# Up's weight sums in place, and a fixed VectorE order in the last part of a two-layer trunk kernel

## The chip, the cores and the metric

The kernel runs on 1 core of one Trainium2 chip. The metric is the device time of one execution in microseconds (us), on the slowest core, which here is the only one. The core's engines are TensorE (PE in the profile, its weight loads PEld), VectorE (DVE), ScalarE (ACT), GpSimd (POOL) and SyncE (SP, which here only starts transfers). Each takes its instructions in the order that the compiler wrote down, and an instruction that waits holds up those behind it.

## The reference

A two-layer decoder trunk over 512 positions of 1024 channels, in float32. Each layer adds a mixer to the residual and then a gated feed-forward part (FFN) to it; a root-mean-square norm stands before each, and one at the end. The change lies in the two FFNs, and in the end of the second:

```
def gated_conv_ffn(x, w_gate, w_up, conv_w, conv_b, w_down):
    g = jnp.einsum('bsd,df->bsf', x, w_gate)
    g = causal_dwconv3(g, conv_w) + conv_b
    up = jnp.einsum('bsd,df->bsf', x, w_up)
    return jnp.einsum('bsf,fd->bsd', jax.nn.silu(g) * up, w_down)
...
    hn = rms_norm(h, norm_ffn[layer])
    h = h + gated_conv_ffn(hn, w_ffn_gate[layer], w_ffn_up[layer], conv_ffn[layer],
                           b_conv_ffn[layer], w_ffn_down[layer])
return rms_norm(h, final_norm)
```

The hidden width is 2816, which is 22 blocks of 128.

## The kernel before, in words

**Three products for one.** Each float32 operand is split into a high part, rounded to TensorE's float32r, and a low part, the rest. A product is then the sum of high by high, high by low and low by high. A split costs a copy on ScalarE (high) and a subtraction on VectorE (low); in another form (`summed`, lines 136 to 145, and `split` in `prepare`, lines 753 to 758) ScalarE writes the negated rounded copy, and a DMA started by GpSimd adds the original to it on its way (`accum_op`), which spares VectorE.

**Seven products for eight.** From block 2 on, the FFN's hidden blocks are made in pairs (f = 2, 4, ..., 20, each f and f+1) by a Winograd scheme: a 2 by 2 product of sub-blocks is done with seven products of sums and differences. `prepare(f)` (line 729) loads four raw tiles (Gate and Up, each in two halves of the input channels; four buffers "raw"), and forms for each of Gate ("g") and Up ("u") two tiles of sums: s12 (lines 744 to 748, for products 5 and 6) and s34 (lines 767 to 769, for products 7 and 3). The tiles of sums carry the tag "sum", which has three slots; the compiler gives a tile a slot once all readers of the tile that had it are done. Each is split into high and low parts (L726 and L727, or for Gate from f = 6 on by ScalarE and the accumulating DMA, L756 to L758). `behind(a, b)` only says that a comes after b on the same engine: the sums of a stage come after the last stage's add of product 7 (`self.added`).

`products(f)` (line 779) then runs fourteen products in the order g1, u1, g5, g2, g6, u5, u6, u2, g7, u7, g3, u3, g4, u4. They accumulate in a few PSUM banks (a, b, e; `BANK`, line 552): product 6 goes on top of product 1 in bank a, so it may start only when ScalarE has copied product 1 out (L810) and, from f = 6 on, where the bank holds two halves, VectorE has added the second half (L798). After g3 and g4 come the scale by the norm's factor (L822), the convolution (`conv`, L610 on ScalarE, two steps L612 on VectorE) and silu (L620), after u4 the gating (L830 to L837).

**Order of stages.** `steps` runs the stages f = 0, 2, 4, ..., 20, and after some of them a half of the down projection of four finished blocks (`half_down`; d in layer 0, dn in layer 1), whose results VectorE adds to the residual (L313 in layer 0, L1181 in layer 1). The stage f = 6 is the first wide one.

**The last part of layer 1** (from line 1201). The last four hidden blocks (rows 18 to 21) go through the down projection by the same seven products, now with the hidden blocks as sums too. The raw weights are b11, b12, b21, b22; `less` forms the differences (L1218; t1 and t2, called dnt in the profile, lie in "sum" slots), and `put` splits each weight operand (`stat`) by ScalarE and an accumulating DMA (tiles whi_dnp and wlo_dnp). `block` (line 1233) splits the activations' operands: blocks 1 and 2 are the rows a11 and a12, blocks 5 and 6 the sums s1 and s2 (called dns), blocks 3, 7 and 4 come from a12, a21 and a22 (high on ScalarE, low on VectorE, L1237 to L1243). The products run in the order that the calls of `taken` have: each is six matmuls into a bank followed by VectorE's add to y (L1181). Products 1, 6, 7 and 4 of one half of the tokens share a bank, so product 6 waits for the add after product 1. `inorder` keeps an instruction in the order of the program among the others on its engine that are marked so; everything else the compiler places by its own reckoning. Then come squares, roots and the final scale, row block by row block, and the output DMAs.

Of the kernel before, what the change touches and what calls it, by code (L numbers as in the profile page):

```python
# [8 lines left out]
F32 = mybir.dt.float32  # L9
F32R = mybir.dt.float32r  # L10
BF16 = mybir.dt.bfloat16
AF = mybir.ActivationFunctionType
ALU = mybir.AluOpType
PSUM = bass.MemoryType.PSUM

P = 128
D = 1024
S = 512
# [3 lines left out]
NF = FF // P  # L22
# [9 lines left out]
def tile_trunk(ctx: ExitStack, tc: tile.TileContext, x, norm_mix, norm_ffn, final_norm,  # L32
# [3 lines left out]
    nc = tc.nc  # L36
    x = x[0]
# [45 lines left out]
    def behind(ins, first):  # L83

        if first is not None:
            tc.add_manual_dep(ins.ins, first.ins.name, mybir.DependencyInfo(
                mybir.DependencyClass.NoSync, mybir.DependencyReason.DATA), reason="order")
# [500 lines left out]
    class Ffn:  # L588
# [10 lines left out]
        def __init__(self, layer, prm, norm, ap, sums):  # L599
            self.layer, self.prm, self.ap, self.acts = layer, prm, ap, {}  # L600
            self.norm, self.sums = norm, sums
            self.t23, self.t41, self.t41both = {}, {}, {}
            self.first_sums = None
            self.added = {"g": None, "u": None}
            self.cols = small[:, 3 * PAD : 3 * PAD + NT]

        def conv(self, t, ft):
            ap, prm, n = self.ap, self.prm, f"{self.layer}_{ft}"
            c = ap.tile([P, S], F32, tag="c", bufs=2, name=f"c{n}")
            nc.scalar.activation(c, t[:, 0:S], AF.Copy, scale=prm("cf", ft))  # L610
            for i in (1, 2):
                nc.vector.scalar_tensor_tensor(c, t[:, i : S + i], prm("cf", i * NF + ft), c,  # L612
                                               op0=ALU.mult, op1=ALU.add)
            return c

        def silu(self, c, ft):
            name = f"s{self.layer}_{ft}"
            s = (self.ap.tile([P, S], F32, tag="s", bufs=3, name=name) if ft % 2 else
                 tp.tile([P, S], F32, tag="sq", name=name))
            nc.scalar.activation(s, c, AF.Silu, bias=self.prm("bf", ft))  # L620
            return s

        def act(self, ft, s):
# [105 lines left out]
        def prepare(self, f):  # L729
# [11 lines left out]
                put(key, 1, w, i)  # L741
            for key in "gu":
                r0, r1 = raws[key, 0][0], raws[key, 1][0]
                s12, s34 = (ap.tile([P, 2, 4, P], F32, tag="sum", bufs=3, name=f"{x}{key}_{n}")
                            for x in ("s12", "s34"))
                behind(nc.vector.tensor_tensor(s12[:, 0], r0[:, :, P:], r1[:, :, P:], ALU.add),
                       self.added[key])
                nc.vector.tensor_tensor(s12[:, 1], s12[:, 0], r0[:, :, :P], ALU.subtract)
# [404 lines left out]
    def ffn1(norm):  # L1153
        with tc.tile_pool(name="f1", bufs=1) as ap:
# [59 lines left out]
            def put(product, how, src, **kw):  # L1214
                stat[product] = how(src, 2, 512, f"dnp{product}", **kw)

            def less(dst, x, y_):
                behind(nc.vector.tensor_tensor(dst, x, y_, ALU.subtract), ffn.added["u"])  # L1218

            less(t1, b12, b11)  # L1220
            put(1, summed, b11)
            put(2, summed, b21)
            less(t2, b22, t1)
            put(5, summed, t1)
            put(6, summed, t2)
            less(b12, b22, b12)
            put(3, summed, b22)
            put(7, summed, b12)
            less(b21, b21, t2)

            blocks = {}

            def block(product, n, srcs, after=None):
                hi, lo = (x.rearrange("p (a b) -> p a b", a=2) for x in hg[n])
                blocks[product] = hi, lo
                if not isinstance(srcs, list):
                    ins = nc.scalar.activation(hi, srcs, AF.Copy)  # L1237
                    behind(nc.vector.tensor_tensor(lo, srcs, hi.bitcast(F32), ALU.subtract), after)
                    return ins
                for i, src in enumerate(srcs):  # L1240
                    ins = nc.scalar.activation(hi[:, i], src, AF.Copy)
                    behind(nc.vector.tensor_tensor(lo[:, i], src, hi[:, i].bitcast(F32),
                                                   ALU.subtract), after)  # L1243
                return ins

            a11, a12 = ([rows[a + 2 * i + n][:, :HALF] for n in range(2)] for i in range(2))
            a21, a22 = ([rows[a + 2 * i + n][:, HALF:] for n in range(2)] for i in range(2))
            s1, s2 = (ap.tile([P, 2, HALF], F32, tag="c", bufs=2, name=f"dns{i}") for i in (1, 2))
            block(1, 0, a11)
            block(2, 1, a12)  # L1250
            for n in range(2):
                nc.vector.tensor_tensor(s1[:, n], a21[n], a22[n], ALU.add)
            block(5, 4, s1)
            for n in range(2):
                nc.vector.tensor_tensor(s2[:, n], s1[:, n], a11[n], ALU.subtract)
            put(4, summed, b21, after=block(6, 5, s2))
            banks = {}

            def product(p, i, c0=0, c1=512, bank=None):
# [53 lines left out]
                queue.dma_start(out[t * P : (t + 1) * P, cs], dst)  # L1313


            first_add = taken(1, 0, left)
            for n in range(2):
                nc.vector.tensor_tensor(a12[n], a12[n], s2[:, n], ALU.subtract)
            last_split = block(3, 6, a12, first_add)
            for n in range(2):  # L1320
                nc.vector.tensor_tensor(a21[n], a11[n], a21[n], ALU.subtract)
            block(7, 2, a21, first_add)
            block(4, 3, a22, first_add)

            first_root = work("sd", 1, "first")
            behind(nc.scalar.activation(first_root, eps, AF.Sqrt), last_split)

            taken(1, 1, left)
            taken(2, 0, left)
            taken(5, 0, right)  # L1330
            squared(0, left)
            times(vec, 0, left)
            halved(0, left, True)
# [55 lines left out]
    n = mixer0()  # L1389
# [33 lines left out]
```

## Time and profile before

| what | value |
|---|---|
| time, median of 3 runs | 981.55 us (981.4 to 983.6) |
| the profiled execution's own time | 982.37 us |
| its span in the trace | 980.7 us |
| TensorE busy | 966.7 us (99%), granted clock 0.997 of full |
| VectorE busy | 815.2 us (83%), 1379 instructions |
| ScalarE busy | 593.8 us (61%) |
| GpSimd busy | 144.3 us (15%) |
| end of the last matmul | about 973.3 us |
| DMA | 146.01 MB, mean 149 GB/s |

The span is the profile's time from first to last record; some 1.7 us of the execution lie outside it. Matmul ends are modelled, so a busy TensorE says that matmuls were under way, and gaps show as idle time with the instruction that ended the wait. A row of the timeline has the start, the time taken, the engine, the line, the operation, the tile written and the tiles read, the shapes, the count, and in brackets the idle time of the engine before it with what released it.

### The profile page before, as it was taken

How to read it: one execution, taken by the hardware profiler on the slowest of the kernel's cores; microseconds unless marked ns; L12 is line 12 of the kernel's file. 1: busy time of each engine (PE TensorE's matmuls, PEld its weight loads, DVE VectorE, ACT ScalarE, POOL GpSimd, SP SyncE). 2: the span in 40 equal slices, each digit the busy share in tenths (PEclk: the TensorE clock that was granted, in tenths of full speed). 3: DMA queues.
4: the chain of work that ended last, by engine and by line, in shares of the span. 5: the costliest groups of instructions: out<-in, count | busy, mean ns of one | idle time of the engine just before them, and what ended most of it. 6: DMA issues, size and time to landing. Idle time of an engine off the chain costs nothing.

```text
span 980.7 us, 14161 instructions
## 1 busy us (share of the span) xinstructions
PE 966.7 (99%) x5200; PEld 832.1 (85%) x5200; DVE 815.2 (83%) x1379; ACT 593.8 (61%) x899; POOL 144.3 (15%) x167
## 2 busy tenths in 40 slices
PE   9999999999999999999999999999999999999996
PEld 7888888997888888888889988889978888888884
DVE  5887459979899898998987765489898989889887
ACT  5523347674676565765488734586765566655675
POOL 2141023010111010110310001310111011100122
PEclk9999999999999999999999999999999999999998
DMA  7442226566777678774324623265766877667774
GB/s 249 146 136 86 87 87 139 136 149 158 193 164 185 145 172 193 165 188 127 121 61 113 212 68 105 56 141 134 180 162 163 199 171 185 149 159 196 190 159 124
DMA packets 93554, 146.01 MB, mean 149 GB/s; under 512 B 5060, under 2 KB 60076, under 8 KB 93484
## 3 DMA queue, kind: packets, MB, share of 16 engines
q1 hardware_dynamic: 78316, 98.69, 32.0%
q0 software_dynamic: 13392, 44.57, 25.7%
q10 hardware_dynamic: 1776, 1.84, 0.6%
q8 instruction: 41, 0.67, 0.3%
q14 instruction: 29, 0.24, 0.1%
HBM read 98.42 MB, written 2.10 MB: 103 GB/s over the span
## 4 chain that ended last, share of the span: by engine, by line
PE 86%; DVE 5%; DMA 4%; issue 3%; POOL 0%; ACT 0%; POOLq 0%; DVEq 0%; ACTq 0%
DMA wlo_s12g<-s12g 3%; PE d L157 3%; PE d L156 3%; PE d L155 3%; PE dn L156 2%; PE dn L157 2%; PE dn L155 2%; PE gu L155 2%; PE gu L157 1%; PE oo L157 1%; PE gu L156 1%; PE oo L156 1%; PE oe L156 1%; PE oe L155 1%; PE oo L155 1%
## 5 line engine op out<-in xcount | busy, mean ns | idle before, releaser
L612 DVE SCALAR_TENSOR_TENSOR c<-rows,prm,c 128x512 f32<-128x512 f32 x88 | 65.4, 746 | 3.8 <-ACT c L610 3.6
L142 POOL DMA_DIRECT2D wlo_g<-raw_g x20 | 17.2, 862 | 341.1 <-ACT wlo_g L140 175.1
L156 PE MATMUL dn<-wlo_dn,a_hi 128*128 128x512 f32 x144 | 56.2, 390 | 0.0
L157 PE MATMUL dn<-whi_dn,a_lo 128*128 128x512 f32 x144 | 56.2, 390 | 0.0
L156 PE MATMUL d<-a_lo,whi_d 128*128 128x512 f32 x144 | 56.2, 390 | 0.0
L157 PE MATMUL d<-a_hi,wlo_d 128*128 128x512 f32 x144 | 56.1, 390 | 0.0
L155 PE MATMUL d<-a_hi,whi_d 128*128 128x512 f32 x144 | 56.1, 390 | 0.0
L155 PE MATMUL dn<-whi_dn,a_hi 128*128 128x512 f32 x144 | 56.1, 389 | 0.0
L726 ACT ACTIVATE whi_a<-raw_g 128x512 fp32r<-128x512 f32 x20 | 12.6, 632 | 61.6 <-PE g_6e L567 8.5
L620 ACT ACTIVATE s<-c,prm 128x512 f32<-128x512 f32 x44 | 31.4, 719 | 16.1 <-DVE c L612 16.1
L211 POOL TENSOR_TENSOR ssq_f<-ssq_f,sq_f 128x512 f32<-128x512 f32 x14 | 19.4, 1388 | 134.6 <-ACT sq_f L210 99.7
L200 ACT ACTIVATE hg<-h,prm 128x512 fp32r<-128x512 f32 x24 | 17.3, 722 | 35.0 <-DVE h L313 35.0
L610 ACT ACTIVATE c<-rows,prm 128x512 f32<-128x512 f32 x44 | 31.3, 713 | 2.9 <-DVE rows L822 2.8
L201 DVE SCALAR_TENSOR_TENSOR hg<-h,prm,hg 128x512 fp32r<-128x512 f32 x24 | 23.6, 987 | 11.1 <-ACT hg L200 11.1
L157 PEld LDWEIGHTS dn<-whi_dn,a_lo 128*128 128x128 f32 x144 | 27.0, 188 | 5.7
L157 PEld LDWEIGHTS d<-a_hi,wlo_d 128*128 128x128 f32 x144 | 27.0, 188 | 5.7
L155 PEld LDWEIGHTS dn<-whi_dn,a_hi 128*128 128x128 f32 x144 | 27.0, 188 | 5.4
L156 PEld LDWEIGHTS dn<-wlo_dn,a_hi 128*128 128x128 f32 x144 | 27.0, 188 | 5.4
L155 PEld LDWEIGHTS d<-a_hi,whi_d 128*128 128x128 f32 x144 | 27.1, 188 | 5.4
L156 PEld LDWEIGHTS d<-a_lo,whi_d 128*128 128x128 f32 x144 | 27.0, 188 | 5.4
L264 ACT ACTIVATE a_hi<-s 128x512 fp32r<-128x512 f32 x40 | 24.8, 627 | 10.8 <-PE d L157 7.2
L151 DVE TENSOR_TENSOR wlo_dn<-raw_dn,whi_dn 128x1024 fp32r<-128x1024 f32 x18 | 22.0, 1224 | 11.0 <-ACT whi_dn L150 10.9
(1129 smaller groups left out, 3329.6 us busy)
## 6 DMA issues: line engine op xcount, KB each, us to landing
raw_g<-in_w_ffn_gate_dram SPq DMA_DIRECT2D x40, 512.0 KB, 4.6
raw_u<-in_w_ffn_up_dram SPq DMA_DIRECT2D x40, 512.0 KB, 3.8
raw_dn<-in_w_ffn_down_dram SPq DMA_DIRECT2D x22, 512.0 KB, 6.4
wlo_u<-raw_u POOLq DMA_DIRECT2D x21, 512.0 KB, 7.7
wlo_g<-raw_g POOLq DMA_DIRECT2D x20, 512.0 KB, 4.6
raw_d<-in_w_ffn_down_dram SPq DMA_DIRECT2D x18, 512.0 KB, 5.8
wlo_s12g<-s12g POOLq DMA_DIRECT2D x16, 512.0 KB, 6.8
wlo_s34g<-s34g POOLq DMA_DIRECT2D x16, 512.0 KB, 6.0
```

The lines of the kernel that those rows point to most:

```text
L142: nc.gpsimd.dma_start(lo, raw, accum_op=ALU.add)
L151: behind(nc.vector.tensor_tensor(lo, raw, hi.bitcast(F32), ALU.subtract), after[0])
L155: nc.tensor.matmul(ps, lhs[0], rhs[0], start=start, stop=False)
L156: nc.tensor.matmul(ps, lhs[0], rhs[1], start=False, stop=False)
L157: nc.tensor.matmul(ps, lhs[1], rhs[0], start=False, stop=stop)
L200: nc.scalar.activation(hg[k][0], h[k], AF.Copy, scale=g)
L201: nc.vector.scalar_tensor_tensor(hg[k][1], h[k], g, hg[k][0].bitcast(F32), op0=ALU.mult, op1=ALU.subtract)
L211: nc.gpsimd.tensor_tensor(self.ssq, self.ssq, sq, ALU.add)
L264: nc.scalar.activation(hi, src, AF.Copy, scale=scale)
L610: nc.scalar.activation(c, t[:, 0:S], AF.Copy, scale=prm("cf", ft))
L612: nc.vector.scalar_tensor_tensor(c, t[:, i : S + i], prm("cf", i * NF + ft), c, op0=ALU.mult, op1=ALU.add)
L620: nc.scalar.activation(s, c, AF.Silu, bias=self.prm("bf", ft))
```

## The change

In `prepare`, Up's s34 is no tile of its own: it is s12 itself, so its two sums are written over s12's two halves once those have been split. A stage then takes three tiles with the tag "sum" instead of four. In the last part: product 6's weight split is put behind the last silu, and the difference that goes into b21 behind the last convolution step (both were behind the last stage's add); blocks 2, 5, 6 and 3 and the differences for s2 and for a12 are marked `inorder` on VectorE; block 5's and block 6's low parts come after the first and second adds of product 1; the differences for a12 and a21 and the low parts of blocks 3, 7 and 4 come after four adds instead of one, and the marks that held the latter behind the first add are gone. The matmuls and their order are the same.

```diff
@@ class Ffn
+            self.last_conv = self.last_silu = None
...
             for i in (1, 2):
-                nc.vector.scalar_tensor_tensor(c, t[:, i : S + i], prm("cf", i * NF + ft), c,
-                                               op0=ALU.mult, op1=ALU.add)
+                self.last_conv = nc.vector.scalar_tensor_tensor(
+                    c, t[:, i : S + i], prm("cf", i * NF + ft), c, op0=ALU.mult, op1=ALU.add)
...
-            nc.scalar.activation(s, c, AF.Silu, bias=self.prm("bf", ft))
+            self.last_silu = nc.scalar.activation(s, c, AF.Silu, bias=self.prm("bf", ft))
...
-                s12, s34 = (ap.tile([P, 2, 4, P], F32, tag="sum", bufs=3, name=f"{x}{key}_{n}")
-                            for x in ("s12", "s34"))
+                s12 = ap.tile([P, 2, 4, P], F32, tag="sum", bufs=3, name=f"s12{key}_{n}")
+                s34 = s12 if key == "u" else ap.tile([P, 2, 4, P], F32, tag="sum", bufs=3,
+                                                     name=f"s34{key}_{n}")
@@ ffn1
-            def less(dst, x, y_):
-                behind(nc.vector.tensor_tensor(dst, x, y_, ALU.subtract), ffn.added["u"])
+            def less(dst, x, y_, after=None):
+                behind(nc.vector.tensor_tensor(dst, x, y_, ALU.subtract), after or ffn.added["u"])
...
-            put(6, summed, t2)
+            put(6, summed, t2, after=ffn.last_silu)
             less(b12, b22, b12)
             put(3, summed, b22)
             put(7, summed, b12)
-            less(b21, b21, t2)
+            less(b21, b21, t2, ffn.last_conv)
...
-            def block(product, n, srcs, after=None):
+            def block(product, n, srcs, keep=lambda ins: ins):
...
+                for hi, lo, src in pairs:
+                    ins = nc.scalar.activation(hi, src, AF.Copy)
+                    keep(nc.vector.tensor_tensor(lo, src, hi.bitcast(F32), ALU.subtract))
                 return ins
+
+            def minus(dst, x, y_, keep=lambda ins: ins):
+                for n in range(2):
+                    keep(nc.vector.tensor_tensor(dst[n], x[n], y_[n], ALU.subtract))
...
             block(1, 0, a11)
-            block(2, 1, a12)
             for n in range(2):
                 nc.vector.tensor_tensor(s1[:, n], a21[n], a22[n], ALU.add)
-            block(5, 4, s1)
-            for n in range(2):
-                nc.vector.tensor_tensor(s2[:, n], s1[:, n], a11[n], ALU.subtract)
-            put(4, summed, b21, after=block(6, 5, s2))
+            s1_, s2_ = ([x[:, n] for n in range(2)] for x in (s1, s2))
+            minus(s2_, s1_, a11, inorder)
+            block(2, 1, a12, inorder)
...
-            first_add = taken(1, 0, left)
-            for n in range(2):
-                nc.vector.tensor_tensor(a12[n], a12[n], s2[:, n], ALU.subtract)
-            last_split = block(3, 6, a12, first_add)
-            for n in range(2):
-                nc.vector.tensor_tensor(a21[n], a11[n], a21[n], ALU.subtract)
-            block(7, 2, a21, first_add)
-            block(4, 3, a22, first_add)
-
+            taken(1, 0, left)
+            block(5, 4, s1, inorder)
+            taken(1, 1, left)
+            put(4, summed, b21, after=block(6, 5, s2, inorder))
+            minus(a12, a12, s2_, inorder)
+            taken(2, 0, left)
+            taken(5, 0, right)
+            last_split = block(3, 6, a12, inorder)
+            minus(a21, a11, a21)
+            block(7, 2, a21)
+            block(4, 3, a22)
             first_root = work("sd", 1, "first")
             behind(nc.scalar.activation(first_root, eps, AF.Sqrt), last_split)
 
-            taken(1, 1, left)
-            taken(2, 0, left)
-            taken(5, 0, right)
             squared(0, left)
```

More of the change, by code (lines that the diff above doesn't have):

```diff
@@ L1228, in ffn1 @@
             put(7, summed, b12)
-            less(b21, b21, t2)
+            less(b21, b21, t2, ffn.last_conv)
             blocks = {}
-            def block(product, n, srcs, after=None):
+            def block(product, n, srcs, keep=lambda ins: ins):
                 hi, lo = (x.rearrange("p (a b) -> p a b", a=2) for x in hg[n])
                 blocks[product] = hi, lo
[L1236 to L1243, printed above, removed]
-                return ins
+                pairs = [(hi[:, i], lo[:, i], src) for i, src in enumerate(srcs)] if (
+                    isinstance(srcs, list)) else [(hi, lo, srcs)]
+                for hi, lo, src in pairs:
+                    ins = nc.scalar.activation(hi, src, AF.Copy)
+                    keep(nc.vector.tensor_tensor(lo, src, hi.bitcast(F32), ALU.subtract))
+                return ins
+            def minus(dst, x, y_, keep=lambda ins: ins):
+                for n in range(2):
+                    keep(nc.vector.tensor_tensor(dst[n], x[n], y_[n], ALU.subtract))
             a11, a12 = ([rows[a + 2 * i + n][:, :HALF] for n in range(2)] for i in range(2))
```

## The prediction

> **What bounds the kernel now.** I read the page's first part, then TensorE's list of waits, then the busy time of stretches between stage starts, then VectorE's waits and the timeline where TensorE stood.
>
> ```profile
> PE 966.7 (99%) x5200; PEld 832.1 (85%) x5200; DVE 815.2 (83%) x1379; ACT 593.8 (61%) x899; POOL 144.3 (15%) x167
> PE g_6a L567 <- DVE rows L798: 3.3, 2, 1.8
> PE dn_a L1271 <- DVE y L1181: 1.7, 2, 1.0
> ```
>
> TensorE is busy 966.7 of 980.7 us, so only its gaps can be won, and both large waits are for VectorE: 3.3 us in two waits of product g_6a, 1.7 us in two waits of the last part's bank a. The change touches no matmul; it can only move those waits. The waits understate the first loss, since matmul ends are modelled, so I take the length of whole stages, from one stage's first matmul to the next's:
>
> ```profile
> 219.45:252.54 33.09, 31.04 (x162) 26.20 (x160) 31.77 (x58) 18.96 (x29) 2.93 (x4) 1.00 0.61 148
> 252.54:283.42 30.88, 30.78 (x162) 26.23 (x160) 26.91 (x51) 18.84 (x29) 3.04 (x4) 1.00 0.73 182
> 283.42:314.26 30.84, 30.76 (x162) 26.23 (x160) 29.24 (x54) 20.73 (x30) 4.72 (x6) 1.00 0.81 191
> 314.26:344.81 30.55, 30.55 (x162) 26.18 (x161) 27.06 (x50) 18.07 (x28) 2.37 (x3) 1.00 0.67 161
> 705.66:737.90 32.24, 30.76 (x161) 26.08 (x160) 30.09 (x56) 20.01 (x30) 3.82 (x5) 1.00 0.77 185
> ```
>
> (Columns: stretch, its length, busy time of TensorE, weight loads, VectorE, ScalarE, GpSimd, clock, DMA share, GB/s.) These are stages f=6, 8, 10, 12 of layer 0 and f=6 of layer 1. An undisturbed stage takes 30.55. So f=6 loses 33.09 - 30.55 = 2.54 us in layer 0 and 32.24 - 30.55 = 1.69 in layer 1; f=8 and f=10 of layer 0 lose 0.33 + 0.29 = 0.62. With the last part's 1.7 that is 6.55 us, the most that this change can bring.
>
> **Up's sums in place.** Now four tiles a stage (s12g, s34g, s12u, s34u) share three slots, so s34u takes the slot of s12g and waits until s12g's accumulating DMA has landed:
>
> ```profile
> DVE s34u L767 <- DMA wlo_s12g<-s12g: 11.0, 7, 2.6
> DVE wlo_dn L151 <- ACT whi_dn L150: 10.9, 12, 1.1
> ```
>
> Most of those seven waits are covered. At f=6 they are not. From the timeline, VectorE in layer 0 and one row of layer 1, then TensorE in both (start, time, instruction, count, and in brackets the idle time before it and what ended it):
>
> ```profile
> 220.15 0.69 DVE L767 TENSOR_TENSOR s34u<-raw_u 128x512 f32<-128x512 f32 x1 [2.63 <-DMA wlo_s12g<-s12g]
> 220.76 0.75 DVE L612 SCALAR_TENSOR_TENSOR c<-rows,prm,c 128x512 f32<-128x512 f32 x1
> ...
> 225.09 1.22 DVE L727 TENSOR_TENSOR wlo_s12u<-s12u,whi_s12u 128x1024 fp32r<-128x1024 f32 x1
> 226.22 1.29 DVE L266 TENSOR_TENSOR a_lo<-s,a_hi 128x512 fp32r<-128x512 f32 x2
> 227.42 0.68 DVE L769 TENSOR_TENSOR s34u<-raw_u,s12u 128x512 f32<-128x512 f32 x1
> 228.02 0.42 DVE L798 TENSOR_TENSOR rows<-g_6a,rows 128x256 f32<-128x256 f32 x1
> ...
> 705.51 0.69 DVE L767 TENSOR_TENSOR s34u<-raw_u 128x512 f32<-128x512 f32 x1 [1.78 <-DMA wlo_s12g<-s12g]
> ```
>
> ```profile
> 228.59 1.15 PE L567 MATMUL g_6a<-t,whi_s12g 128*128 128x512 f32 x4 [1.85 <-DVE rows L798]
> ...
> 713.59 1.17 PE L567 MATMUL g_6a<-t,whi_s12g 128*128 128x512 f32 x4 [1.48 <-DVE rows L798]
> ```
>
> VectorE works in order. It stands 2.63 us before s34u's first sum, with the convolution, the residual adds, the gating and at last the add L798 queued behind; from 220.15 it runs without a hole to that add at 228.02, and product 6 of Gate, which accumulates onto the bank that the add reads, starts only at 228.59. Removed: the DMA wait. In place, s34u's first sum needs no free slot; it needs both readers of s12u, ScalarE's high copy and VectorE's low part (1.22), both of which the stage does anyway, so no instruction is added. Without the wait the same run of work brings the add's end from 228.44 to 225.81. TensorE could have begun the product at 228.59 - 1.85 = 226.74, so the cover is 0.93 us and the whole 2.54 can go. I take 2.1, because s34u now also stands behind wlo_s12u and may pull that 1.22 ahead of the add: bounds 0 (all of the wait is replaced) and 2.54. Layer 1: the add comes 1.78 earlier against a wait of 1.48; I take 1.5, bounds 0 and 1.69. Nearest row for the upper end is the stall itself, so I stay near it.
>
> The new wait has its own price. Stage f=10 of layer 0 shows it:
>
> ```profile
> 286.33 0.68 DVE L767 TENSOR_TENSOR s34u<-raw_u 128x512 f32<-128x512 f32 x1
> 286.93 0.69 DVE L769 TENSOR_TENSOR s34u<-raw_u,s12u 128x512 f32<-128x512 f32 x1
> 287.54 1.23 DVE L727 TENSOR_TENSOR wlo_s12u<-s12u,whi_s12u 128x1024 fp32r<-128x1024 f32 x1
> 288.68 0.42 DVE L798 TENSOR_TENSOR rows<-g_10a,rows 128x256 f32<-128x256 f32 x1
> ```
>
> Here both s34u sums lie exactly in the time in which ScalarE makes the high copy of s12u. In place they cannot: between the last s12u sum, which ends the row before these, and L727 there is a hole of 287.54 - 286.33 = 1.21 us. If the add L798 fills it, it comes 288.68 - 286.33 = 2.35 earlier and the small stalls of f=8 and f=10 (0.62) go; if nothing fills it, the add comes 1.21 later and TensorE, which has no slack there, pays 1.21 in each such stage (f=8, f=10 and the like; I count three). I take +0.4, bounds +0.62 and -3.6 (3 x 1.21). The add is ready by then, and nothing older can run in that hole, so filling is the likelier end.
>
> What else hangs on s34u: its low parts are ready later by at most the hole and the two sums, 1.21 + 1.21 = 2.4 us; its first matmul (u, 7) is the tenth of fourteen products, so this is hidden unless ScalarE's copies out of PSUM queue behind whi_s34u. The raw Up blocks come free later by as much, and SyncE's next load behind them too; it is a Gate block of the next stage, a stage ahead. Both at 0; uncovered, they cost one to one. The three slots are now taken by three tiles, so the next s12g meets a slot freed a stage ago: 0.
>
> **The last part.** From the timeline, VectorE, TensorE and ScalarE; then one stretch, and how long the transfers out of the tiles dnt took:
>
> ```profile
> 945.60 1.23 DVE L1218 TENSOR_TENSOR raw_dn<-raw_dn,dnt 128x1024 f32<-128x1024 f32 x1 [1.73 <-issue]
> ...
> 957.08 0.74 DVE L1181 SCALAR_TENSOR_TENSOR y<-dn_a,small,y 128x512 f32<-128x512 f32 x1
> 957.74 2.14 DVE L1242 TENSOR_TENSOR hg<-s,hg 128x256 fp32r<-128x256 f32 x6
> 959.80 0.74 DVE L1181 SCALAR_TENSOR_TENSOR y<-dn_a,small,y 128x512 f32<-128x512 f32 x1
> ```
>
> ```profile
> 957.97 0.47 PE L1271 MATMUL dn_a<-whi_dnp,hg 128*128 128x512 f32 x1 [0.64 <-DVE y L1181]
> ...
> 960.60 0.50 PE L1271 MATMUL dn_a<-whi_dnp,hg 128*128 128x512 f32 x1 [1.02 <-DVE y L1181]
> ```
>
> ```profile
> 943.38 1.05 ACT L140 ACTIVATE wlo_dnp<-dnt 128x1024 fp32r<-128x1024 f32 x1
> ...
> 949.12 0.72 ACT L620 ACTIVATE s<-c,prm 128x512 f32<-128x512 f32 x1 [0.33 <-DVE c L612]
> ```
>
> ```profile
> 950.00:960.00 10.00, 8.94 (x39) 6.79 (x37) 10.00 (x24) 9.14 (x16) 1.73 (x2) 1.00 0.71 135
> ```
>
> ```profile
> DMA to landing us min/median/max: 5.6/5.9/6.3
> ```
>
> TensorE stands 0.64 and 1.02 us, first for the add of product 1's first half at 957.08, then for that of its second half at 959.80. Ahead of the first stood a hole of 1.73 us before the difference L1218 and that difference itself (1.23); between the two stand six low parts (2.14). The change puts L1218 behind the last convolution step, puts the first add ahead of the low parts of 5 and 6 and of the differences for 3 and 7, and leaves only one low part between the two adds. The order alone moves work from before these adds to after them; VectorE's sum of work stays. So at most the hole of 1.73 is won, and TensorE can win 0.64 + 1.02 = 1.66. From above the two agree. I take 1.2: the fixed order can itself make VectorE stand for a ScalarE copy, and the nearest row for that is the wlo_dn wait, 1.1 at longest, so the lower bound is -1.1. The end after the last matmul is unchanged.
>
> Moved too: product 6's split now starts behind the last silu instead of at 943.38. That silu ran at 949.12, and comes earlier by up to 1.73 + 1.23 = 2.96 (the hole and the L1218 go behind its convolution), so the split starts near 949.12 + 0.72 - 2.96 = 946.9; with 1.05 for the low copy and 6.3 at worst for the landing it is there by 954.3, ahead of product 6 at 957.97 - 0.64 = 957.33. Cover 3.1 us; without it, TensorE waits one to one. ScalarE's queue gets that work after the silu, which is why the silu is early; GpSimd's transfers of 3, 7 and 4 are queued behind it, and their products follow product 6 in the matmul order. No DMA on SyncE's queue is moved here.
>
> One rule of the Trainium skill speaks against this term. The stretch 950 to 960 has VectorE at 10.00 of 10.00 and TensorE at 8.94. The page "Perfetto Trace Analysis", section "Identifying the Most-Contended Engine", says that the engine with the highest occupancy is the one to relieve; by it VectorE binds here, moving its work without removing any brings 0, and the whole sum would be 4.0. The row of 1.73 us speaks against it: that VectorE was full after a hole that it need not have had.
>
> **The sum.** 2.1 + 1.5 + 0.4 + 1.2 = 5.2 us. The profiled execution took 982.37 (span 980.7 and 1.7 around it), so it would take 977.2; the median of the runs is 0.82 lower, 981.55, so I predict 981.55 - 5.2 = 976.4. All bounds at their best give 2.54 + 1.69 + 0.62 + 1.66 = 6.5, 975.0.
>
> **Rivals.** (a) VectorE remains the bound in the last part: after 957 it has as much to do as before and the adds only swap places. The last term is 0: 981.55 - 4.0 = 977.6. For it the 10.00 of 10.00; against it the hole. (b) The f=6 stall stays: wlo_s12u and both s34u sums, older in program order than the add, now run ahead of it, and the add still ends after 227. Only the last part and a little more is won: 981.55 - 1.2 = 980.3. It decides if more than the cover of 0.93 us is put in front of the add. (c) Slower: VectorE held in order by ScalarE's high copy of s12u, with the add behind it. Nothing fills the hole after L748, three stages of layer 0 pay 1.21 each, the same order keeps the f=6 stalls, and the last part's fixed order makes VectorE wait for the high copies likewise, so that it wins nothing: 981.55 + 3.6 = 985.2. It decides as soon as the add comes any later than now in f=8 and f=10, since both stages already lose 0.3 us. Against it: the add waits only for ScalarE's copy out of the bank, which comes before the hole opens. (d) It does not do what it says: the compiler orders VectorE anew around the shared tile and the waits only change their names: 981.5.
>
> **Chances.** Forecast 0.50, (a) 0.13, (b) 0.20, (c) 0.09, (d) 0.08. A measurement of this kernel can tell about 0.3%, 2.9 us, from no change. Faster by more than that: forecast and (a), 0.63; within: (b) and (d), 0.28; slower: (c), 0.09. The range goes from all bounds at their best, with 0.2 for error, 974.8, up to just past (d), 981.7.
>
> **What would show it.** Right: no wait of s34u for wlo_s12g; s34u's first sum after wlo_s12u in every stage; f=6 stages at 30.6 to 31.2 us; adds of g_8a and g_10a before wlo_s12u; no wait of dn_a for the y adds above 0.3 us; last matmul about 5 us earlier, and as much from it to the end. Wrong: f=6 still over 32 us, layer 0's later stages over 31 us, or a new wait of dn_a for wlo_dnp.

## The result and the profile after

The changed kernel takes 975.71 us (975.47 to 976.67, six runs) against 981.79 us (981.4 to 983.6, six runs): a ratio of 0.9937, interval 0.9924 to 0.9950, so 6.1 us less. Run again later, beside the last of the experiments, it was 976.44 against 981.57: ratio 0.9948, interval 0.9935 to 0.9960. The ratios here are estimates over all executions and can differ a little from the quotient of the two medians. The profiled execution took 976.67 us, its span is 974.8 against 980.7 before.

First the busy times from the page of the changed kernel, then the whole list of what TensorE waited for (us in total, times, longest):

```profile
PE 965.1 (99%) x5200; PEld 832.2 (85%) x5200; DVE 813.6 (83%) x1379; ACT 592.0 (61%) x899; POOL 144.6 (15%) x167
```

```profile
PE clock L61 <- DVE idle L56: 1.3, 1, 1.3
PE dn_a L1272 <- DVE y L1183: 0.9, 1, 0.9
```

No engine does noticeably more or less than before. The two waits of g_6a (3.3 us) are gone, and the last part's bank a has one wait of 0.9 where it had two of together 1.7. The first row is the start of the program, the same in both. Then the stretches that were shown of before, by their new times, with f=14 of layer 0 (the fourth row) and the last part, from the first matmul of product 1 to the last matmul (the sixth):

```profile
219.37:249.87 30.50, 30.50 (x161) 26.17 (x160) 29.68 (x55) 18.97 (x28) 2.89 (x4) 1.00 0.67 161
249.87:280.42 30.55, 30.55 (x162) 26.18 (x160) 26.50 (x50) 18.20 (x29) 2.58 (x3) 1.00 0.73 180
280.42:310.96 30.54, 30.54 (x161) 26.17 (x160) 28.18 (x53) 19.70 (x29) 4.30 (x5) 1.00 0.68 156
341.51:372.53 31.02, 30.87 (x161) 26.29 (x160) 28.09 (x53) 19.69 (x30) 4.22 (x5) 1.00 0.67 153
702.59:733.14 30.55, 30.55 (x162) 26.17 (x160) 28.16 (x53) 19.76 (x29) 3.81 (x5) 1.00 0.73 178
946.96:967.45 20.49, 19.63 (x91) 15.85 (x89) 18.86 (x45) 14.63 (x32) 7.12 (x6) 1.00 0.56 125
```

and of before the two that the prediction did not show, f=14 of layer 0 and the last part:

```profile
344.81:375.47 30.66, 30.66 (x161) 26.23 (x160) 28.82 (x54) 20.63 (x30) 4.53 (x6) 1.00 0.80 184
951.73:973.32 21.59, 19.93 (x91) 15.73 (x89) 20.24 (x48) 14.97 (x33) 7.11 (x6) 1.00 0.43 101
```

So f=6 of layer 0 gains 33.09 - 30.50 = 2.59, f=6 of layer 1 32.24 - 30.55 = 1.69, f=8 and f=10 of layer 0 0.33 and 0.30, and the last part 21.59 - 20.49 = 1.10. The stage f=18 of layer 0 goes from 30.67 to 30.54 (0.13), and f=14 loses 31.02 - 30.66 = 0.36. Together 2.59 + 1.69 + 0.63 + 1.10 + 0.13 - 0.36 = 5.78 of the 5.9 us between the spans; of the rest, 219.45 - 219.37 = 0.08 lies ahead of the first of these stages.

Next, VectorE at f=6 of layer 0 after the change:

```profile
221.64 1.22 DVE L728 TENSOR_TENSOR wlo_s12u<-s12u,whi_s12u 128x1024 fp32r<-128x1024 f32 x1
222.77 1.28 DVE L266 TENSOR_TENSOR a_lo<-s,a_hi 128x512 fp32r<-128x512 f32 x2
223.98 0.68 DVE L769 TENSOR_TENSOR s12u<-raw_u 128x512 f32<-128x512 f32 x1
224.58 0.68 DVE L771 TENSOR_TENSOR s12u<-raw_u,s12u 128x512 f32<-128x512 f32 x1
225.18 0.41 DVE L800 TENSOR_TENSOR rows<-g_6a,rows 128x256 f32<-128x256 f32 x1
```

No row has a bracket: VectorE waits for nothing. Both sums now write s12u after its low part. The add that frees bank a ends at 225.59, 6.22 us into the stage; before it was 228.44, 8.99 into it. Product 6 starts without a wait. At f=10:

```profile
283.39 0.68 DVE L750 TENSOR_TENSOR s12u<-s12u,raw_u 128x512 f32<-128x512 f32 x1
284.00 0.42 DVE L800 TENSOR_TENSOR rows<-g_10a,rows 128x256 f32<-128x256 f32 x1
285.20 1.22 DVE L728 TENSOR_TENSOR wlo_s12u<-s12u,whi_s12u 128x1024 fp32r<-128x1024 f32 x1 [0.79 <-ACT whi_s12u L727]
...
286.75 0.68 DVE L769 TENSOR_TENSOR s12u<-raw_u 128x512 f32<-128x512 f32 x1
```

The add has moved into the time in which ScalarE makes the high copy; what is left of the hole is 0.79. In the last part, VectorE and the one wait of TensorE:

```profile
941.63 1.21 DVE L1220 TENSOR_TENSOR raw_dn<-raw_dn,dnt 128x1024 f32<-128x1024 f32 x1
...
948.52 0.75 DVE L1183 SCALAR_TENSOR_TENSOR y<-dn_a,small,y 128x512 f32<-128x512 f32 x1 [0.28 <-PE dn_a L1272]
949.19 0.68 DVE L1242 TENSOR_TENSOR hg<-dns,hg 128x512 fp32r<-128x512 f32 x1
949.88 0.75 DVE L1183 SCALAR_TENSOR_TENSOR y<-dn_a,small,y 128x512 f32<-128x512 f32 x1
...
954.61 1.42 DVE L1242 TENSOR_TENSOR hg<-s,hg 128x256 fp32r<-128x256 f32 x4
955.95 0.68 DVE L1308 TENSOR_TENSOR yf<-y,fin 128x512 f32<-128x512 f32 x1
956.56 0.14 DVE L1295 TENSOR_SCALAR ssf<-ssf 128x1 f32<-128x1 f32 x1
956.62 1.39 DVE L1183 SCALAR_TENSOR_TENSOR y<-dn_a,small,y 128x512 f32<-128x512 f32 x2
```

```profile
957.50 0.47 PE L1272 MATMUL dn_a<-whi_dnp,hg 128*128 128x512 f32 x1 [0.86 <-DVE y L1183]
```

The hole of 1.73 us before the difference L1220 is gone, and both adds of product 1 (948.52 and 949.88) now come as soon as their products are done. The wait of 0.9 that is left is a new one: the add of product 6's first half at 956.62 stands behind the low parts of blocks 7 and 4 and the first multiply of the final scale, and product 7, in the same bank, waits 0.86 for it.

### The profile page after: what moved, and what is told of

It reads as the page before. It is cut to its first block, busy times and chain, and to the rows that moved or that the text cites. A ratio compares the mean times of both kernels' runs of the same rounds, so it can differ in the third digit from the quotient of the medians.

```text
span 974.8 us, 14101 instructions
## 1 busy us (share of the span) xinstructions
PE 965.1 (99%) x5200; PEld 832.2 (85%) x5200; DVE 813.6 (83%) x1379; ACT 592.0 (61%) x899; POOL 144.6 (15%) x167
## 4 chain that ended last, share of the span: by engine, by line
PE 93%; DVE 4%; DMA 1%; issue 1%; ACT 0%; POOLq 0%; DVEq 0%; SPq 0%; POOL 0%
PE dn L156 3%; PE dn L157 3%; PE dn L155 3%; PE d L156 3%; PE d L157 3%; PE d L155 3%; PE gu L155 2%; PE gu L157 2%; PE oo L155 1%; PE gu L156 1%; PE oo L156 1%; PE oe L157 1%; PE oe L156 1%; PE oo L157 1%; PE oe L155 1%; PE u_4a L577 1%
## 5 line engine op out<-in xcount | busy, mean ns | idle before, releaser
L1183 DVE SCALAR_TENSOR_TENSOR y<-dn,small,y 128x512 f32<-128x512 f32 x40 | 27.7, 746 | 6.3 <-PE dn L157 6.3
L728 DVE TENSOR_TENSOR wlo_s34u<-s12u,whi_s34u 128x1024 fp32r<-128x1024 f32 x20 | 24.5, 1223 | 7.2 <-ACT whi_s34u L727 6.8
```

The costliest lines, as they stand in the source:

```text
L728: nc.vector.tensor_tensor(lo, src, hi.bitcast(F32), ALU.subtract)
L1183: return nc.vector.scalar_tensor_tensor(dst, ps, ffn.cols[:, t : t + 1], dst, op0=ALU.mult, op1=ALU.add)
```

## The experiments

What each run was to tell apart is quoted ahead of what it measured. "Last part" is always the stretch from product 1's first matmul to the last matmul.

**Up's sums alone.** The kernel before, with this one edit:

```diff
-                s12, s34 = (ap.tile([P, 2, 4, P], F32, tag="sum", bufs=3, name=f"{x}{key}_{n}")
-                            for x in ("s12", "s34"))
+                s12 = ap.tile([P, 2, 4, P], F32, tag="sum", bufs=3, name=f"s12{key}_{n}")
+                s34 = s12 if key == "u" else ap.tile([P, 2, 4, P], F32, tag="sum", bufs=3,
+                                                     name=f"s34{key}_{n}")
```

> Only Up's in-place sums; the last part as before. If the two halves of the change act each by itself (theory): the stages gain what they gained in the changed kernel, 2.59 (f=6, layer 0) + 0.33 + 0.30 + 0.13 - 0.36 (the new stall at f=14) + 1.69 (f=6, layer 1) = 4.7 us, so a span about 4.7 below the before's and about 977.0 us; the f=14 stage of layer 0 shows 31.0 and its wait of the Gate sum for a load, the last part 0.64 + 1.02 of waits as before. If the fixed order in the last part changes earlier stages too, or the last part's gain needs the earlier sums: another split, with the stages under 4 or over 5.5 us.

Measured: 977.55 us against 981.62, ratio 0.9959 (0.9946 to 0.9971). Its stretches f=6 and f=14 of layer 0 and the last part:

```profile
219.47:249.97 30.50, 30.50 (x161) 26.17 (x160) 29.68 (x55) 18.97 (x28) 2.89 (x4) 1.00 0.64 161
341.61:372.16 30.55, 30.55 (x162) 26.17 (x160) 29.09 (x53) 20.45 (x30) 4.54 (x6) 1.00 0.70 167
946.79:968.41 21.62, 19.95 (x91) 15.73 (x89) 20.28 (x48) 15.02 (x33) 7.13 (x6) 1.00 0.43 101
```

The stages behave as in the changed kernel and the last part as before the change, so the two halves act each by itself. One point was missed: f=14 does not stall here.

**The last part alone.** The changed kernel with the four tiles of sums put back (the edit above undone).

> Only the last part's order; four tiles of sums in each stage as before. Theory: every stage up to the last part is as before (f=6 33.1 and 32.2), and the last part alone gains the 1.1 us that it gained in the changed kernel: about 980.6 us. Rival (VectorE is the bound of the last part, so an order gives nothing): 981.7, a last part as long as before. Third: part of the 1.1 belongs to the Up change; then less than 1.1 here.

Measured: 981.56 us (980.05 to 983.15) against 981.62, ratio 0.9998 (0.9989 to 1.0007). Its f=6 of layer 0, and its last part:

```profile
219.17:252.46 33.29, 31.25 (x161) 26.22 (x160) 31.75 (x58) 18.94 (x29) 2.91 (x4) 1.00 0.59 147
952.01:972.50 20.49, 19.62 (x91) 15.87 (x89) 18.86 (x45) 14.64 (x32) 7.12 (x6) 1.00 0.56 124
```

The stretch gives the answer and the total does not: the last part is 20.49, 1.10 shorter, exactly as in the changed kernel, while the expected 980.6 did not come. The interval of the ratio just reaches down to the 1.1 us (0.9989). The executions of this kernel lie 3.1 us apart, and the stall at f=6 is one thing that differs between executions (its size is taken up below).

**A fourth slot, and its control.** The kernel before with one more slot for the sums. To make room, another tile (rstd) has one buffer instead of two; the control has only that.

```diff
-                s12, s34 = (ap.tile([P, 2, 4, P], F32, tag="sum", bufs=3, name=f"{x}{key}_{n}")
+                s12, s34 = (ap.tile([P, 2, 4, P], F32, tag="sum", bufs=4, name=f"{x}{key}_{n}")
...
-            r = tp.tile([P, S], F32, tag="rstd", name=f"rstd_{self.name}")
+            r = tp.tile([P, S], F32, tag="rstd", bufs=1, name=f"rstd_{self.name}")
```

> The kernel before with a fourth slot for the sums and no tile used in place; a slot is won by giving one other tile one buffer instead of two. If the stall of the two f=6 stages is the wait for a slot (theory): both stages at 30.5 and a gain of 4.2 to 4.5 us, near 977.4; the small stalls of f=8, 10 and 18 in layer 0 (0.3, 0.3, 0.1) stay, as the sums stand ahead of the adds still, and the f=14 stall of the changed kernel (0.36) does not come, as raw Up blocks come free as early as before. If the gain came from the order in which VectorE meets sums and adds and not from the slot: f=6 stays at 33 and 32, no gain.

> Control of the run with four slots: only the one tile's buffers cut from two to one, three slots as before. Theory: nothing waits for the second buffer, 981.7 +- 0.5, stages as before. Rival: it costs a start-up or statistics wait, and then the run with four slots carries the same cost.

Measured: four slots 977.84 us, ratio 0.9962 (0.9949 to 0.9976); the control 982.06, ratio 1.0005 (0.9995 to 1.0014). With four slots, f=6 and f=8 of layer 0, then f=6 of layer 1; below it the first two of the control:

```profile
219.31:250.07 30.76, 30.75 (x161) 26.25 (x160) 28.20 (x54) 19.24 (x30) 3.12 (x5) 1.00 0.67 162
250.07:280.62 30.55, 30.55 (x162) 26.19 (x160) 27.52 (x51) 18.43 (x29) 3.02 (x4) 1.00 0.74 189
702.65:733.19 30.54, 30.54 (x161) 26.12 (x160) 26.88 (x51) 19.33 (x29) 3.26 (x5) 1.00 0.74 180
```

```profile
219.22:251.46 32.24, 30.74 (x162) 26.18 (x160) 31.61 (x58) 18.95 (x29) 2.92 (x4) 1.00 0.60 152
251.46:282.00 30.54, 30.54 (x161) 26.18 (x160) 26.95 (x51) 18.89 (x29) 3.07 (x4) 1.00 0.75 186
```

A free slot takes the stall away, and the control without it does not. So the wait for the slot was the cause at f=6. The program's order is untouched here, but with a slot free the compiler places VectorE's work anew: both of Up's sums come ahead of the stage (215.14 and 215.74), and the add that frees bank a stands behind the low part of the second pair of sums too. It ends 6.89 us into the stage, against 6.22 with Up in place. That order is the likely source of the remainder, 30.76 - 30.50 = 0.26 at f=6, and of about 0.1 each at f=10, f=14 and f=18 of layer 0, which are 30.62, 30.67 and 30.66 here and 30.55, 30.55 and 30.54 with Up in place; no run tries it by itself. One point was missed: f=8 was to keep its loss and has none. The control also shows that this loss is not in every execution: with three slots it has f=8 at 30.54, not 30.88.

**The fixed order alone.** The kernel before with only the later edits of the last part: the blocks and differences marked in order, and the adds among them, as in the changed kernel.

```diff
-            put(6, summed, t2, after=ffn.last_silu)
+            put(6, summed, t2)
-            less(b21, b21, t2, ffn.last_conv)
+            less(b21, b21, t2)
```

(against the run "the last part alone")

> The kernel before with only the later half of the last part's edits: blocks, differences and adds in the fixed order, and the split of product 6's weights and its last difference where they stood before. Theory (the two waits of the last part, 0.64 for the add of product 1 and 1.02 later, go by the order of the adds, and 0.86 of a new wait comes by product 7's first half): the gain is 1.66 - 0.86 = 0.8, about 980.9 us. Rival (VectorE's hole ahead of the fixed order was what made everything late): under 0.3 here, and the gain comes with the run that moves only the two weight steps.

**The two weight steps alone.** The kernel before with the other half:

```diff
-            put(6, summed, t2)
+            put(6, summed, t2, after=ffn.last_silu)
...
-            less(b21, b21, t2)
+            less(b21, b21, t2, ffn.last_conv)
```

> The kernel before with only the two moved weight steps: product 6's split behind the last silu, the last difference behind the last convolution. Theory: VectorE's hole closes, but the adds keep their old places, so the wait of product 2 for the add of product 1 stays near 0.64; the gain is between 0 and 0.6, about 981.4 us. Rival (the hole is the cause of both waits): 1.1 or more, about 980.6.

Measured: the order alone 981.37 us against 982.15, ratio 0.9998 (0.9987 to 1.0008); the weight steps alone 979.80 against the same 982.15, ratio 0.9977 (0.9968 to 0.9986). The last part of the order alone and TensorE's wait in it, then the same two of the weight steps alone:

```profile
952.90:974.36 21.46, 19.82 (x91) 15.77 (x89) 20.17 (x48) 15.10 (x33) 7.12 (x6) 1.00 0.44 101
```

```profile
964.37 0.50 PE L1271 MATMUL dn_a<-whi_dnp,hg 128*128 128x512 f32 x1 [1.64 <-DVE y L1182]
```

```profile
950.39:970.41 20.02, 19.69 (x91) 15.79 (x89) 18.66 (x45) 14.42 (x32) 7.12 (x6) 1.00 0.57 127
```

```profile
957.68 0.50 PE L1271 MATMUL dn_a<-whi_dnp,hg 128*128 128x512 f32 x1 [0.33 <-DVE y L1181]
```

My theory fell and the rival held. The order alone wins 21.59 - 21.46 = 0.13: its two waits become one of nearly the same sum. The two weight steps alone win 21.59 - 20.02 = 1.57, which is 0.47 more than the whole change wins there. So the two weight steps, which close the hole, are worth 1.57 in the last part, and the fixed order, put on top, takes 0.47 of it back.

**What made the hole.** The profile shows only "issue" for it. GpSimd's row of before, and then GpSimd's and VectorE's rows of the run with Up's sums alone, which kept the hole:

```profile
940.05 0.86 POOL L142 DMA_DIRECT2D wlo_dnp<-raw_dn  x1 [1.03 <-ACT rows L810]
```

```profile
935.11 0.86 POOL L142 DMA_DIRECT2D wlo_dnp<-raw_dn  x1 [1.04 <-ACT rows L811]
940.68 1.23 DVE L1219 TENSOR_TENSOR raw_dn<-raw_dn,dnt 128x1024 f32<-128x1024 f32 x1 [1.76 <-issue]
```

The accumulating DMA of product 2 reads the raw tile b21, and the difference writes into that same tile. In before the difference starts 945.60 - 940.05 = 5.55 us after that DMA was issued, here 940.68 - 935.11 = 5.57; in the run with the order alone it is 5.56 and in the run with the split alone, below, 5.55. The longest landing of the transfers out of this tile in before is 5.5. In the changed kernel it is 941.63 - 935.28 = 6.35, and there is no wait. By these times the difference stood at the head of VectorE's queue until a transfer had read its tile. That four kernels agree within 0.02 us is strong, but the release itself is not in the records, so this is argued and not shown.

**Only the split moved.** Up in place, product 6's split behind the last silu, the difference free:

```diff
-            less(b21, b21, t2, ffn.last_conv)
+            less(b21, b21, t2)
```

(against the run "Up in place and the two weight steps", which comes next)

> As the run before, but of the two weight steps only the split of product 6's sum is moved; the last difference stays free. Theory (the difference stood in VectorE's queue and waited, idle for 1.73, for ScalarE's split of the same tile; with the split late but the difference free, VectorE's wait gets longer or the difference goes by itself behind the convolutions): if the split alone is the cause, a last part of 20.0 to 20.3; if the place of the difference is, 21.6 or more, about 976.8.

Measured: 978.46 us against 981.57, ratio 0.9967 (0.9955 to 0.9979); the last part is 22.57 and the hole 1.75. The split moved without the difference leaves the hole as it was. So the place of the difference counts; no run moves the difference alone, so whether it would do without the split is open. The split alone makes things 0.95 worse than Up's sums alone (21.62): ScalarE, without that work, first stands 3.48 us for VectorE, and does the split when the high copies of the activations are due, so that TensorE now waits for ScalarE too, 0.55 and 0.17 us, beside 1.22 for an add.

**Up in place and the two weight steps.** Both, without the fixed order.

> Up's sums in place and the two moved weight steps, without the fixed order of blocks and adds. Theory (the hole cost the last part its 1.57 us, the fixed order gives 0.47 of it back): the last part is 20.02 as in the run with the two weight steps alone, against 20.49 of the changed kernel, the stages as in the changed kernel: 0.47 less than the repeat of the changed kernel on this chip, about 975.2. Rival (with Up in place VectorE comes to the last part in another order, and the fixed order is needed): no gain or a loss against the repeat.

**The changed kernel again**, on the same chip.

> The changed kernel once more, for a second profile and to stand on the same chip as the next three. If the stall of 0.36 in the stage f=14 of layer 0 is a price of the later free load buffers in every execution: that stage shows 31.0 again. If it belongs to one execution in which VectorE came 1.3 us late into the stage: 30.55 here, and a span near 974.3. The last part 20.49 either way, the f=6 stages 30.5.

Measured: 975.72 us (975.54 to 976.36) without the order, 976.44 (976.08 to 976.62) for the changed kernel; ratios to before 0.9941 (0.9929 to 0.9954) and 0.9948 (0.9935 to 0.9960). The last part of the former, and f=14 of layer 0 and the last part of the latter:

```profile
946.65:966.65 20.00, 19.68 (x91) 15.81 (x89) 18.66 (x45) 14.45 (x32) 7.11 (x6) 1.00 0.57 128
```

```profile
341.76:372.31 30.55, 30.55 (x162) 26.17 (x160) 28.98 (x54) 20.60 (x30) 4.71 (x6) 1.00 0.71 168
946.77:967.26 20.49, 19.63 (x91) 15.85 (x89) 18.86 (x45) 14.63 (x32) 7.12 (x6) 1.00 0.56 125
```

Without the fixed order the last part is 0.49 shorter, and the medians are 0.72 apart the same way; five executions each, whose ranges overlap by 0.28, so the trace carries this better than the times. It has the lowest median of the kernels run on that chip. The f=14 stall of 0.36 did not come back.

**Two tries to mend the remaining wait.** In the changed kernel, the adds of product 6 earlier:

```diff
             block(7, 2, a21)
+            taken(6, 0, right)
             block(4, 3, a22)
...
             squared(0, left)
+            taken(6, 1, right)
             times(vec, 0, left)
             halved(0, left, True)
-            taken(6, 0, right)
-            taken(6, 1, right)
```

> The changed kernel with the adds of product 6 ahead of the last block's subtraction and the final scale. Theory: the 0.86 us that product 7's first half waits for that add goes, and the last part with it: 974.9 us. Rival (product 4's block is then late by the two adds, or the scale's multiply ends the kernel): the wait moves to product 4 or to the end and no more than 0.2 is won, 975.6.

In the kernel without the fixed order, the second add of product 1 ahead of the low parts of block 4:

```diff
-            block(4, 3, a22, first_add)
+            block(4, 3, a22, taken(1, 1, left))
...
-            taken(1, 1, left)
```

> As the run with Up in place and both weight steps moved, with the second add of product 1 put ahead of the splitting of product 4's lows. Theory: the one wait left in the last part, 0.33 for that add behind six pieces of lows (2.10 together), goes, as two of the six (0.67) come after the add: a last part of 19.7, and 0.3 less than the run without it. Rival: the wait moves to the next product's add or to the lows of product 4, and the last part stays 20.0.

Measured: 976.23 us, ratio 0.9940 (0.9927 to 0.9952), last part 20.40; and 975.86, ratio 0.9943 (0.9930 to 0.9955), last part 20.60. Neither theory held. The first moved the wait of 0.86 to a later matmul in bank a, where it is 0.64, and its last part is 0.09 shorter, as the rival said. The second made of one wait of 0.32 two, of 0.23 (dn_a) and 0.43 (dn_e), and its last part is 0.60 longer than the 20.00 without it, which is worse than its rival.

**The price of an add behind the sums.** The changed kernel, with the first Gate add of the stages after f=6 tied behind Up's last sum:

```diff
+                self.last_sum = nc.vector.tensor_tensor(s34[:, 1], r1[:, :, :P], s12[:, 1],
+                                                        ALU.subtract)
...
-                    add(d, bank, halves[1:])
+                    ins = add(d, bank, halves[1:])
+                    if (key, product) == ("g", 1) and f > FIRST_WIDE:
+                        behind(ins, self.last_sum)
```

> The changed kernel with the first Gate add of each stage after f=6 forced behind both of Up's last sums. It tries the price of the rival on the slower side: if the add lies in the hole by luck of the order and the stage has no slack, each of f=8, 10, 14 and 18 of layer 0 loses up to 1.2 us, in all 3 to 5 us, about 979 to 980.5; layer 1's stages lose little. If the banks have slack for the add (the add of f=8 in layer 0 came after the splitting of the lows and nothing waited): under 0.5 us, about 976.0.

Measured: 978.37 us (978.03 to 980.04), ratio 0.9965 (0.9953 to 0.9978). Its f=10, f=14 and f=18 of layer 0:

```profile
280.08:311.16 31.08, 30.77 (x161) 26.16 (x160) 28.94 (x54) 19.65 (x29) 4.21 (x5) 1.00 0.65 158
341.85:373.32 31.47, 30.80 (x161) 26.15 (x160) 29.31 (x55) 19.99 (x29) 4.30 (x5) 1.00 0.63 158
403.87:434.95 31.08, 30.78 (x161) 26.16 (x160) 29.03 (x54) 19.63 (x29) 4.19 (x5) 1.00 0.65 158
```

Between the two expectations: against 30.55, the three lose 0.53, 0.92 and 0.53, f=12 loses 0.14 and f=8 (30.55) nothing, in all 2.1 us. At f=10 the add starts 7.23 us into the stage instead of 3.58; it comes 3.65 later for 0.53. But TensorE's order is not the same here. Its rows at f=10, some left out:

```profile
285.67 1.09 PE L567 MATMUL u_10e<-t,whi_s12u 128*128 128x512 f32 x4
...
287.78 1.19 PE L567 MATMUL g_10a<-t,whi_s12g 128*128 128x512 f32 x4 [0.32 <-DVE rows L801]
```

At f=10, f=14 and f=18, the three stages that lose most, the compiler put product 5 of Up and one matmul of its product 6 ahead of product 6 of Gate, which waits for the add; in before and in the changed kernel product 6 of Gate comes first. These nine matmuls cover most of the delay. Without such cover there is next to none: the run with four slots and the five profiles with four tiles in three slots keep the order of before at f=10, their add ends 5.49, 5.64, 5.68, 5.88, 5.89 and 5.99 us into the stage, and the stage loses 0.07, 0.25, 0.29, 0.49, 0.50 and 0.62 against 30.55. From 5.49 on each 0.1 of delay costs about 0.1.

## Why the prediction was right, point by point

**The sum.** By its terms it said 2.1 + 1.5 + 0.4 + 1.2 = 5.2, and 2.59 + 1.69 + 0.40 + 1.10 = 5.78 were won.

**What bounds the kernel: right.** The time that TensorE lost was nearly the whole account (5.78 of 5.9); VectorE's and ScalarE's busy times hardly changed.

**f=6: right in its mechanism, a little small.** It said 2.1 and 1.5, and 2.59 and 1.69 were won. The fear behind the discount, that the low part of s12u would be pulled ahead of the add, did not apply: the prediction's own rows have it ahead already (225.09 against the add at 228.02), and there is room for it and both sums. The run with a fourth slot shows that it is the slot. What the prediction could not see from one profile is that the term has no fixed size. In the five profiles of kernels with four tiles in three slots, VectorE's wait in layer 0 was 1.78, 1.79, 2.14, 2.63 and 2.85, and the stage 32.26, 32.24, 34.17, 33.09 and 33.29. The profile of before had one of the long ones.

**f=8 and f=10: the sum 0.4 met by luck, its reason right only in part.** f=8, f=10 and f=18 gave 0.33 + 0.30 + 0.13, and f=14 took 0.36, which the prediction had at 0; that the net is 0.40 is chance. The add does fill the hole at f=10. Of the 0.29 lost there before, four slots with the old order take away 0.22; why VectorE is earlier there is not shown. At f=8, where I had the add ahead of the low part of s12u too, it comes behind it, and nothing is lost. The loss at f=8 came not from the two sums but from a wait for the slot of its own. VectorE's rows there, in before and in the control:

```profile
255.56 0.69 DVE L767 TENSOR_TENSOR s34u<-raw_u 128x512 f32<-128x512 f32 x1 [2.13 <-DMA wlo_s12g<-s12g]
```

```profile
253.86 0.70 DVE L767 TENSOR_TENSOR s34u<-raw_u 128x512 f32<-128x512 f32 x1 [1.51 <-ACT rows L810]
```

In the five profiles with four tiles in three slots VectorE's wait at this place is 2.13 and 2.28 where f=8 takes 30.88 and 31.02, and 1.44 to 1.51 where it takes 30.54 or 30.55. The transfer is issued 4.20 to 4.23 us ahead of the stage in all five, so the long stall at f=6 in the same two profiles did not delay it. From its issue to the end of the wait pass 7.24 and 7.37 us in these two and at most 6.55 to 6.63 in the others, where ScalarE ended two of the three waits. So this loss belonged to the term of the slot.

**The price of an unfilled hole: right for one order of the matmuls only.** The step "TensorE, which has no slack there, pays 1.21 in each such stage" holds for the order of before: there an add that ends later costs about one to one, as the six profiles at f=10 show. But with the add tied behind the sums the compiler did not keep that order, and the add, 3.65 us later than in the changed kernel at f=10, cost 0.53 there, and 0.92 and 0.53 in two other stages. What rival (c) left out is that TensorE's order may follow; whether it would have lost its 3.6 us is open, and the run speaks for less.

**"SyncE's next load behind them too … Both at 0": right in most executions.** In one of seven profiles with Up in place and the adds free, f=14 lost time: the Gate load that is issued behind the sums came too late. Its rows, VectorE's and SyncE's:

```profile
359.02 0.69 DVE L748 TENSOR_TENSOR s12g<-raw_g,raw_g 128x512 f32<-128x512 f32 x1 [2.07 <-DMA raw_g<-in_w_ffn_gate_dram]
359.63 0.42 DVE L800 TENSOR_TENSOR kept<-u_14a,kept 128x256 f32<-128x256 f32 x1
```

```profile
353.76 0.37 SPq L130 DMA_DIRECT2D raw_g<-in_w_ffn_gate_dram  x1
```

The load is issued 12.25 us into f=14, against 9.86 before, 5.26 us pass from its issue to the sum, and the add of u_14a stands behind the sum that waits for it: 0.36 us. In the second profile it is issued at 11.48, the sum comes 3.88 after that and waits 0.70, and nothing is lost. Before, the same sum waited 0.82 in a stage of 30.66. So the cover is real but thin. In another of the seven (only the split moved) f=10 takes 30.78: VectorE is 0.44 later there, the add of u_10a ends 12.69 us into the stage, and product 7 of Up starts at 12.74 instead of 12.60.

**The last part: 1.2 forecast, 1.10 won, for another reason.** I wrote that "the change puts L1218 behind the last convolution step", which is what counts, and bounded the gain by the hole of 1.73. But I gave the fixed order its share, where it costs 0.47, and expected "no wait of dn_a for the y adds above 0.3 us", where there is one of 0.86. The two weight steps alone gave 1.57 of the 1.66 that TensorE could win: the bound was right, and the value at it would have been right for the two weight steps. That my discount for the fixed order had about the true size is luck: I gave as its reason that VectorE would stand for a copy of ScalarE, and the trace has the add of product 6 behind low parts and a multiply instead. The cover of product 6's split held: TensorE never waits for wlo_dnp.

**Rival (a) and the full engine.** In the stretch of the last part that had VectorE at 10.00 of 10.00 and TensorE at 8.94, the run with the two weight steps alone has, from the same distance to product 1:

```profile
948.66:958.66 10.00, 9.67 (x43) 7.72 (x42) 10.00 (x21) 9.44 (x17) 2.58 (x3) 1.00 1.03 193
```

VectorE is as full as before, TensorE is at 9.67, and the last part is 1.57 us shorter. By the Trainium skill's page "Perfetto Trace Analysis", section "Identifying the Most-Contended Engine", the engine with the highest occupancy is the one to relieve; over this stretch the trace does not agree, since nothing was taken from VectorE as a whole and 1.57 us were won. With the hole closed VectorE is still full in this stretch; it has come further by then, and 18.66 us of its work fall into the last part instead of 20.24.

**The rivals.** (b) and (d) are excluded by the f=6 stages, (c) by the adds at f=10, (a) by the last part. The forecast of 976.4 stands beside 975.71 in the first runs and 976.44 in the later ones.

## What to carry to other kernels

In these runs a rotating tile made its next owner wait for an accumulating DMA that still read the old one (2.63 us at f=6), and the raw tile that is rewritten in place in the last part seems to have made its writer wait the same way (1.73); look for the instruction at the head of an engine's queue that waits for a transfer, and count what stands behind it. An edit in several parts is to be taken apart on the chip even where its sum came out as forecast: here one half of the last part's edits won 1.57 us, and the other half gave back 0.47. Tying one instruction down can move others: before a run is read as the price of a delay, see whether the compiler kept the order on the engine that was to wait. Where executions of one kernel lie 3 us apart, compare the stretches of the trace that the edit touches rather than the totals.

## What the runs showed of the hardware

The accumulating DMA of s12g at f=6 of layer 0, issued by GpSimd, is not equally long in every execution. From its issue to the end of VectorE's wait it took 6.30, 6.31, 6.67, 7.15 and 7.37 us in five profiles, and the stage grew with it; a wait on such a transfer puts its scatter into the kernel's time. In one profile (the order alone) the granted clock was 0.95 in this one stage and 1.00 in the others listed here. Within the stage it was 0.50 from 229.0 to 232.0 us, just behind a stand of TensorE of 1.85 us that ended at 228.14. The other four have stands of 1.50 to 1.85 at this place and a clock of 1.00, so the stand alone does not make the dip, and one profile does not show its cause. In the profile with the dip, TensorE's busy time in the stage was 32.32 against 30.74 to 31.25 in the other four, which goes a long way to explain why that stage, with a wait of only 2.14, was the longest at 34.17.
